# One 128x128 score product per block in the heads of gated linear attention

## The chip, the cores and the metric

The kernel runs on one core of one Trainium2 chip. The metric is the device time of one execution in microseconds, the median of several runs. TensorE (PE) multiplies matrices, VectorE (DVE), ScalarE (ACT) and GpSimd (POOL) work elementwise, SyncE (SP) issues transfers; each has a queue of its own and works through it in order.

## The reference, cut to what matters

One layer over 512 tokens of 1024 channels: a convolution branch and a branch of gated linear attention, merged, then a feed-forward part. The attention branch has 4 heads, 128 key channels and 256 value channels per head, in chunks of 64 tokens:

```
b = cumsum(gk) in the chunk          # log decay, per key channel
q_dec = q * exp(b);  k_inv = k * exp(-b);  k_end = k * exp(b_last - b)
att  = tril(q_dec @ k_inv.T)         # inside a chunk
o    = att @ v + q_dec @ state       # state: what the chunks before left
state = exp(b_last) * state + k_end.T @ v
o = rmsnorm(o) * silu(r)
```

The rest of the layer (norms, input projection, convolutions, feed-forward) is not touched.

## The kernel before, in words

**Weight products.** Nearly all of TensorE's work is products of the layer's weights in three parts (mm3, L444 to L450: activation low by weight high, high by low, high by high) with 512 tokens moving. A weight tile is loaded by SyncE, its high part made on ScalarE (L355, L385), its low part on VectorE (L356, L390) or, for some tiles, on ScalarE (L387) with an accumulating transfer issued by GpSimd (L388). Two tiles ahead are prepared (`weight`, L408). Pieces of the convolution branch (chains of taps on VectorE and ScalarE, L784 to L806) are put between weight tiles by `fill` (L428). A scheduler orders each engine's queue from the program.

**The heads.** The attention works on blocks of 128 tokens, two chunks each, four blocks. The loop (L1232) runs five rounds: a round prepares head h (decays, queries, keys) and finishes head h-1 (scores, states, outputs), with a weight product between each two of these steps; the outputs of head h-2 are turned and gated (`gated`, L1080) inside the scores of head h-1.

- `decays` (L990): a scan gives b, one buffer that all heads share; e = exp(b), inv = exp(-b), end = exp(b_last - b), three scratch tiles of 512 columns from a pool that rotates through 6 buffers (tag tmp). ea and eb are copies of e at the ends of the first and second chunk of each block (L1002, L1003), dec their product (L1004).
- `queries` (L1006): the tile q holds 4 slots of 64 per block. Slots 0 and 2 get q * e of both chunks (L1010), slot 1 the second chunk times ea (L1012). Slots 0 and 1 are the queries against the state before the block, slot 2 the second chunk's own.
- `keys` (L1014): the tile k holds 5 slots per block. Slots 0 and 2 get k * inv (L1017), slots 1 and 4 k * end (L1018), slot 3 slot 1 times eb (L1020). Slots 3 and 4 are the keys at the block's end, for the state.
- `scores` (L1022): four transposes of slots 3 and 4 (L1026) go through PSUM to kt (L1028). Then, per block, a 64x64 product of the first chunk with itself (L1035, keys slot 0, queries slot 0), and a product of both chunks' keys (slots 1 and 2) with the second chunk's queries (slot 2, L1037). All are f32. Two predicated copies (L1040) put the visible part into att: 64 rows by 128 columns, and 64 rows by 64 columns.
- `states` (L1042): three products of kt with v (L1050), summed with dec (L1054, L1057); the fourth block's keys in kt are not read.
- `outputs` (L1060): att with v (L1069), queries slots 0 and 1 with the state (L1071), squares for the norm (L1073), mean (L1075), its root on GpSimd (L500), the scaled output o (L1078). `gated` turns o (L1084), multiplies (L1087) and splits (L894, L895).

PSUM has five banks for weight products (mm) and three for the rest (ax), each set handed out in rotation. `gate_r` (L1092) runs a weight product and a Silu (L1095) between the steps; `spread` (L846, product in L850) and `token_sums` (L839) belong to the norm of the convolution branch and come later.

Of the kernel before, what the change touches and what calls it, by code (L numbers as in the profile page):

```python
# [10 lines left out]
F32 = mybir.dt.float32  # L11
# [3 lines left out]
AF = mybir.ActivationFunctionType  # L15
ALU = mybir.AluOpType

P = 128
D = 1024
T = 512  # L20
NT = T // P
# [54 lines left out]
def trunk_layer(ctx: ExitStack, tc: tile.TileContext, a: dict, out: bass.AP):  # L76
    nc = tc.nc
# [5 lines left out]
    def scoped(name, bufs, side="left"):  # L83
        scope = ExitStack()
        return scope, scope.enter_context(tc.tile_pool(name=name, bufs=bufs, side=side))
# [11 lines left out]
    gla_scope, gp = scoped("gla", 1, "right")  # L97
# [3 lines left out]
    def nm(s):  # L101
        return f"{s}_{next(names)}"

    def heap(dt=F32):
        return hp.tile([P, T], dt, tag="h", name=nm("h"))

    def tmp(n=T):
        return tp.tile([P, n], F32, tag="tmp", name=nm("tmp"), bufs=6)
# [7 lines left out]
    def small(n, tag):  # L116
        return tp.tile([P, n], F32, tag=tag, name=nm(tag), bufs=4)
# [4 lines left out]
    def ax_bank():  # L122
        return ps.tile([P, T], F32, tag="ax", name=nm("ax"), bufs=3)
# [6 lines left out]
    ident = cp.tile([P, P], F32, name="ident")  # L130
# [7 lines left out]
    keep = cp.tile([P, P], U8, name="keep")  # L138
    att = gp.tile([P, NT, P], F32, name="att")
# [98 lines left out]
    kept = {}  # L238
# [169 lines left out]
    def weight(name, j, ahead=LOOK):  # L408
        assert order[used[0]] == (name, j)
        prefetch(1)  # L410
        used[0] += 1
        prefetch(ahead)
        share = {"two": 2.5, "w_glu": RATE + 0.75}.get(name, RATE)

        fill(share + (1.75 if order[min(len(ready), len(order)) - 1] in ADDED else 0))
        return ready[used[0] - 1]
# [35 lines left out]
    def col_tile(w, acts, acc=None, lo=0, hi=T, at={}, ks=range(KT)):  # L452

        if acc is None:
            acc = mm_bank()
        for k in ks:
            s = slice(k * P, (k + 1) * P)
            ah, al = acts[k]
            mm3(acc[:, lo:hi], (w[0][:, s], w[1][:, s]), (ah[:, lo:hi], al[:, lo:hi]), k == 0, k == KT - 1)
            if k in at:  # L460
                at[k]()
        return acc
# [35 lines left out]
    def rsqrt(v, n):  # L498
        r = small(n, "rstd")
        roots_at[:] = [nc.gpsimd.tensor_tensor(r, v, mhalf[:, :n], ALU.pow)]  # L500
        return r
# [6 lines left out]
    def junk(n):  # L508
        return tp.tile([P, n], BF16, tag="junk", name=nm("junk"), bufs=1)
# [42 lines left out]
    start = tc.manual_schedule(engines=START)  # L552
    start.__enter__()
    rows = tp.tile([P, P], F32, tag="gain", name=nm("rows"), bufs=1)[0:KT, :]
# [261 lines left out]
    for k in range(KT):  # L816
# [3 lines left out]
        pa = col_tile(weight("w_glu", 2 * k), acts1)  # L820
        c = heap()
# [104 lines left out]
    rows = slice(32, 32 + RANK)  # L926
# [9 lines left out]
    rows = slice(96, 96 + RANK)  # L936
# [24 lines left out]
    def gl(n, tag, bufs):  # L961
        return gp.tile([P, n], F32, tag=tag, name=nm(tag), bufs=bufs)

    G16 = 1.0 / 16.0
    QS = float(np.float32(DK**-0.5))
    C = 64
    oa = [None] * KT

    def chunks(t):
        return t.rearrange("p (a c j) -> p a c j", c=2, j=C)  # L970

    def flat(t, p, i):
        return t[:, p, i : i + 2, :].rearrange("p c j -> p (c j)")

    def by_chunk(t):
        return t.rearrange("p (c j) -> p c j", j=C)

    class Head:
# [11 lines left out]
        def decays(self):  # L990
            b = gl(T, "b", 1)
            nc.vector.tensor_tensor_scan(b, run64, ls[self.h], 0.0, ALU.mult, ALU.add)
            self.e, self.inv, self.end = tmp(), tmp(), tmp()
            nc.scalar.activation(self.e, b, AF.Exp, scale=G16)
            nc.scalar.activation(self.inv, b, AF.Exp, scale=-G16)
            bc = by_chunk(b)
            last = bc[:, :, C - 1 : C].to_broadcast([P, 2 * NT, C])
            nc.vector.tensor_tensor(by_chunk(self.end), last, bc, ALU.subtract)
            nc.scalar.activation(self.end, self.end, AF.Exp, scale=G16)
            ends = chunks(self.e)[:, :, :, C - 1]  # L1000
            self.ea, self.eb, self.dec = small(NT, "ea"), small(NT, "eb"), small(NT, "dec")
            nc.vector.tensor_copy(self.ea, ends[:, :, 0])  # L1002
            nc.vector.tensor_copy(self.eb, ends[:, :, 1])  # L1003
            nc.vector.tensor_tensor(self.dec, self.ea, self.eb, ALU.mult)  # L1004

        def queries(self):  # L1006
            pq = col_tile(weight("w_qk", 2 * self.h), acts1)
            q = self.q = gp.tile([P, NT, 4, C], F32, tag="q", name=nm("q"), bufs=2)
            qc = q.rearrange("p a c j -> p (a c) j")[:, 0::2, :]
            nc.vector.scalar_tensor_tensor(qc, by_chunk(pq), QS, by_chunk(self.e), ALU.mult, ALU.mult)  # L1010
            ea = self.ea.unsqueeze(2).to_broadcast([P, NT, C])
            nc.vector.tensor_tensor(q[:, :, 1, :], q[:, :, 2, :], ea, ALU.mult)  # L1012

        def keys(self):  # L1014
            pk = col_tile(weight("w_qk", 2 * self.h + 1), acts1)
            k = self.k = gp.tile([P, NT, 5, C], F32, tag="k", name=nm("k"), bufs=2)
            nc.vector.tensor_tensor(k[:, :, 0:3:2, :], chunks(pk), chunks(self.inv), ALU.mult)  # L1017
            nc.vector.tensor_tensor(k[:, :, 1:5:3, :], chunks(pk), chunks(self.end), ALU.mult)  # L1018
            eb = self.eb.unsqueeze(2).to_broadcast([P, NT, C])
            nc.vector.tensor_tensor(k[:, :, 3, :], k[:, :, 1, :], eb, ALU.mult)  # L1020

        def scores(self, between=None):  # L1022
            q, k = self.q, self.k
            pt = ax_bank()
            for p in range(NT):
                nc.tensor.transpose(pt[:, p * P : (p + 1) * P], flat(k, p, 3), ident)  # L1026
            self.kt = gl(T, "kt", 1)
            nc.scalar.copy(self.kt, pt)  # L1028
            if between:
                between()  # L1030
            pa = ax_bank()
            pb = pa.rearrange("p (a i) -> p a i", a=NT)

            for p in range(NT):
                nc.tensor.matmul(pb[:C, p, :C], k[:, p, 0, :], q[:, p, 0, :], start=True, stop=True)  # L1035
            for p in range(NT):
                nc.tensor.matmul(pb[:, p, C:], flat(k, p, 1), q[:, p, 2, :], start=True, stop=True)  # L1037
            for rows, cols in ((slice(0, C), slice(0, P)), (slice(C, P), slice(C, P))):
                visible = keep[rows, cols].unsqueeze(1).to_broadcast([C, NT, cols.stop - cols.start])
                nc.vector.copy_predicated(att[rows, :, cols], visible, pb[rows, :, cols])  # L1040

        def states(self):  # L1042

# [16 lines left out]
        def outputs(self):  # L1060
            self.o = tp.tile([P, NT, DV], F32, tag="x", name=nm("o"), bufs=3)
            ss = small(NT, "ss4")
            halves = []
            for p in range(NT):
                if p % 2 == 0:
                    po = ax_bank()
                half = po[:, (p % 2) * DV : (p % 2 + 1) * DV]
                halves.append(half)
                nc.tensor.matmul(half, att[:, p, :], self.v(p), start=True, stop=p == 0)  # L1069
                if p:  # L1070
                    nc.tensor.matmul(half, flat(self.q, p, 0), self.s[p], start=False, stop=True)  # L1071
            for p, half in enumerate(halves):
                nc.scalar.activation(junk(DV), half, AF.Square, scale=1.0 / 16.0, accum_out=ss[:, p : p + 1])  # L1073
            v = small(NT, "mean")
            nc.vector.tensor_scalar(v, ss, EPS, None, ALU.add)  # L1075
            r = rsqrt(v, NT)
            for p, half in enumerate(halves):
                nc.scalar.activation(self.o[:, p, :], half, AF.Copy, scale=r[:, p : p + 1])  # L1078
# [526 lines left out]
    ends = {}  # L1605
# [21 lines left out]
    for gi, pairs in enumerate(GROUPS):  # L1627
        acts = []
        if gi == 0:
# [8 lines left out]
            p, q = pairs[0]  # L1638
# [139 lines left out]
```

## Time and profile before

| | |
|---|---|
| median of 3 runs | 824.66 us (824.33 to 824.96) |
| span of the profiled execution | 822.8 us |
| its own time beside the span | not given apart; the median lies 1.9 us above the span |
| instructions | 11563 |
| scan of the first head to L1084 of the last (the heads) | 149.4 to 284.8 us |
| HBM read, written | 103.42 MB, 2.10 MB |

The span runs from the first to the last instruction that the profiler saw. A row of the chain gives the start, the length that counts until the next step, the engine, the tile, the line and the number of passes. A row of the timeline gives start, duration, engine, line, operation, tile out and in, shapes, and in brackets the idle time ahead with what ended it. A row of groups gives count, total busy time, mean ns of one, and idle time ahead. TensorE's rows carry the form of its tile (128*64 is rows by columns of weights); a duration there includes the way through the pipeline, so the distance of two starts is what a pass costs. An f32 product shows as two passes.

### The profile page before, as it was taken

The numbers are of one execution on the slowest core, as the hardware profiler recorded it, in microseconds if no ns is written. First come the engines' busy times: TensorE is split into PE (matmuls) and PEld (weight loads), VectorE is DVE, ScalarE is ACT, GpSimd is POOL, SyncE is SP. The second block draws the span as 40 slices with busy tenths as digits, with TensorE's granted clock in tenths as the row PEclk, the third lists the DMA queues.
The fourth block names the chain that finished last, engine by engine and source line by source line (L and its number), as shares of the span: only waits on it lengthen the run. The fifth ranks groups of instructions, "written<-read, shape, count | busy, mean of one in ns | idle before, by whom it ended". The sixth has DMA issues, their size and how long they took to land.

```text
span 822.8 us, 11563 instructions
## 1 busy us (share of the span) xinstructions
PE 814.5 (99%) x4323; PEld 703.3 (85%) x4323; DVE 719.0 (87%) x1165; ACT 450.6 (55%) x666; POOL 146.5 (18%) x133
## 2 busy tenths in 40 slices
PE   9999999999999999999999999999999999999996
PEld 7888888888888889999988898898889988899885
DVE  6689999998989699876788889979975999789896
ACT  6643447656564446684445546556435663466654
POOL 2000010001100213532001000230133301612012
PEclk9999999999999999999999999999999999999999
DMA  8355572553432113223547623145632446224662
GB/s 317 104 131 147 146 192 83 129 154 102 106 100 103 51 35 120 103 78 122 206 107 222 192 73 103 45 161 160 141 137 83 147 129 165 105 103 147 186 128 103
DMA packets 30616, 106.27 MB, mean 129 GB/s; under 512 B 3464, under 2 KB 3600, under 8 KB 30560
## 3 DMA queue, kind: packets, MB, share of 16 engines
q1 hardware_dynamic: 24784, 85.34, 29.4%
q0 software_dynamic: 5760, 20.19, 14.1%
q8 instruction: 34, 0.56, 0.3%
q14 instruction: 22, 0.18, 0.1%
q10 hardware_dynamic: 16, 0.00, 0.0%
HBM read 103.42 MB, written 2.10 MB: 128 GB/s over the span
## 4 chain that ended last, share of the span: by engine, by line
PE 98%; DMA 1%; ACT 0%; DVE 0%; POOL 0%; issue 0%; POOLq 0%; SPq 0%; ACTq 0%
PE mm L448 28%; PE mm L449 28%; PE mm L450 28%; PE mm L662 3%; PE ax L450 2%; PE ax L449 2%; PE ax L448 2%; PE ax L1069 1%; PE ax L1071 1%; PE ax L1050 1%; DMA raw<-in_w_v_dram 1%; PE ax L1037 1%; PE ax L529 0%; PE ax L576 0%; PE ax L1035 0%; PE ax L1084 0%
## 5 line engine op out<-in xcount | busy, mean ns | idle before, releaser
L448 PE MATMUL mm<-uh,wlo 128*128 128x512 f32 (+1 forms) x672 | 244.5, 364 | 0.0
L449 PE MATMUL mm<-ul,whi 128*128 128x512 f32 (+1 forms) x672 | 242.3, 361 | 0.0
L450 PE MATMUL mm<-uh,whi 128*128 128x512 f32 (+1 forms) x672 | 242.1, 360 | 0.0
L450 PEld LDWEIGHTS mm<-uh,whi 128*128 128x128 f32 x672 | 126.8, 189 | 19.5
L448 PEld LDWEIGHTS mm<-uh,wlo 128*128 128x128 f32 x672 | 127.0, 189 | 18.8
L449 PEld LDWEIGHTS mm<-ul,whi 128*128 128x128 f32 x672 | 127.0, 189 | 18.6
L385 ACT CAST whi<-raw 128x1024 fp32r<-128x1024 f32 x86 | 89.9, 1048 | 56.2 <-PE mm L450 31.1
L356 DVE TENSOR_TENSOR wlo<-raw,whi 128x1024 fp32r<-128x1024 f32 x80 | 95.2, 1197 | 26.5 <-ACT whi L355 22.4
L327 POOL TENSOR_TENSOR raw<-raw,raw 128x512 f32<-128x512 f32 x42 | 66.7, 1589 | 215.8 <-DVE wlo L356 127.6
L390 DVE TENSOR_TENSOR wlo<-raw,whi 128x1024 fp32r<-128x1024 f32 x70 | 90.0, 1288 | 13.1 <-ACT whi L385 13.1
L355 ACT CAST whi<-raw 128x1024 fp32r<-128x1024 f32 x80 | 76.4, 959 | 36.5 <-PE mm L450 27.3
L788 DVE SCALAR_TENSOR_TENSOR c<-h,pp,c 128x255 f32<-128x255 f32 (+14 forms) x120 | 58.9, 491 | 3.2 <-ACT c L784 3.1
L788 DVE SCALAR_TENSOR_TENSOR c<-aside,btmp,c 128x255 f32<-128x255 f32 (+14 forms) x120 | 58.8, 490 | 0.0
L788 DVE SCALAR_TENSOR_TENSOR aside<-h,pp,aside 128x255 f32<-128x255 f32 (+6 forms) x112 | 54.9, 490 | 0.0
L355 ACT CAST whi<-kept 128x1024 fp32r<-128x1024 f32 (+1 forms) x32 | 31.8, 997 | 30.8 <-DVE kept L310 16.5
L1502 DVE SCALAR_TENSOR_TENSOR tmp<-mm,pp,tmp 128x511 f32<-128x511 f32 (+1 forms) x56 | 41.4, 742 | 4.0 <-ACT tmp L1499 3.9
L356 DVE TENSOR_TENSOR wlo<-kept,whi 128x1024 fp32r<-128x1024 f32 (+1 forms) x32 | 38.0, 1187 | 5.4 <-ACT whi L355 5.4
L1180 ACT COPY tmp<-mm 128x256 f32<-128x256 f32 x48 | 17.7, 369 | 35.9 <-PE mm L450 35.4
L1418 DVE TENSOR_TENSOR hres<-hres,mm 128x512 f32<-128x512 f32 (+1 forms) x49 | 32.3, 672 | 2.8 <-PE mm L450 2.0
L1499 ACT ACTIVATE tmp<-mm,pp 128x512 f32<-128x512 f32 x28 | 21.8, 779 | 19.0 <-PE mm L450 18.8
L387 ACT ACTIVATE wlo<-raw 128x1024 fp32r<-128x1024 f32 x16 | 16.9, 1060 | 22.1 <-PE mm L448 22.1
L1502 DVE SCALAR_TENSOR_TENSOR tmp<-tmp,pp,tmp 128x511 f32<-128x511 f32 (+1 forms) x32 | 27.8, 887 | 0.3
(351 smaller groups left out, 1778.6 us busy)
## 6 DMA issues: line engine op xcount, KB each, us to landing
raw<-in_w_up_dram SPq DMA_DIRECT2D x44, 512.0 KB, 3.6
raw<-in_w_glu_dram SPq DMA_DIRECT2D x16, 512.0 KB, 5.2
raw<-in_w_down_dram SPq DMA_DIRECT2D x15, 512.0 KB, 3.8
kept<-in_w_down_dram POOLq DMA_DIRECT2D x10, 512.0 KB, 5.5
raw<-in_w_v_dram SPq DMA_DIRECT2D x8, 512.0 KB, 5.5
raw<-in_w_qk_dram SPq DMA_DIRECT2D x8, 512.0 KB, 3.3
raw<-in_w_r_dram SPq DMA_DIRECT2D x8, 512.0 KB, 4.5
wlo<-in_w_r_dram POOLq DMA_DIRECT2D x8, 512.0 KB, 8.6
```

The source lines that it names most:

```text
L327: work = nc.gpsimd.tensor_tensor(out, x, y, ALU.add)
L355: nc.scalar.copy(hi, raw)
L356: two_low[:] = [nc.vector.tensor_tensor(lo, raw, hi.bitcast(F32), ALU.subtract)]
L385: nc.scalar.copy(hi, raw)
L390: pace[0] = nc.vector.tensor_tensor(lo, raw, hi.bitcast(F32), ALU.subtract)
L448: nc.tensor.matmul(acc, ll, rh, start=first, stop=False, **kw)
L449: nc.tensor.matmul(acc, lh, rl, start=False, stop=False, **kw)
L450: nc.tensor.matmul(acc, lh, rh, start=False, stop=last, **kw)
L662: nc.tensor.matmul(acc, act, ready[k // 2][wi][:, j], start=first, stop=last)
L788: nc.vector.scalar_tensor_tensor(out[:, j:], x[:, : half_t - j], w, out[:, j:], ALU.mult, ALU.add)
L1418: done = nc.vector.tensor_tensor(hres[t, n][:, c], hres[t, n][:, c], acc[:, c], op)
L1502: nc.vector.scalar_tensor_tensor(z[:, s:], acc[:, : T - s], w[j], z[:, s:], ALU.mult, ALU.add)
```

## The change

For a block's first chunk the queries are now also scaled from the chunk's end: q * exp(b) * exp(-b_last). With these, keys scaled to the first chunk's end serve the queries of both chunks, and one product of 128 keys by 128 queries gives a block's scores. The tile q gets the new slot 0; the old slots 0, 1 and 2 become 1, 2 and 3. The tile k loses the slot of the first chunk's k * inv. inv is computed from the last token of the first chunk on (65 of 128 columns per block). ea and eb are no copies any more but views of e. The keys of the last block are neither scaled for the state nor turned. The two predicated copies become one over 128 rows.

```diff
@@ -972,6 +972,9 @@
     def flat(t, p, i):
         return t[:, p, i : i + 2, :].rearrange("p c j -> p (c j)")
 
+    def by_block(t):
+        return t.rearrange("p (a i) -> p a i", a=NT)
+
     def by_chunk(t):
         return t.rearrange("p (c j) -> p c j", j=C)
 
@@ -992,52 +995,50 @@
             nc.vector.tensor_tensor_scan(b, run64, ls[self.h], 0.0, ALU.mult, ALU.add)
             self.e, self.inv, self.end = tmp(), tmp(), tmp()
             nc.scalar.activation(self.e, b, AF.Exp, scale=G16)
-            nc.scalar.activation(self.inv, b, AF.Exp, scale=-G16)
+            after_half = slice(C - 1, 2 * C)
+            nc.scalar.activation(by_block(self.inv)[:, :, after_half], by_block(b)[:, :, after_half], AF.Exp, scale=-G16)
             bc = by_chunk(b)
             last = bc[:, :, C - 1 : C].to_broadcast([P, 2 * NT, C])
             nc.vector.tensor_tensor(by_chunk(self.end), last, bc, ALU.subtract)
             nc.scalar.activation(self.end, self.end, AF.Exp, scale=G16)
             ends = chunks(self.e)[:, :, :, C - 1]
-            self.ea, self.eb, self.dec = small(NT, "ea"), small(NT, "eb"), small(NT, "dec")
-            nc.vector.tensor_copy(self.ea, ends[:, :, 0])
-            nc.vector.tensor_copy(self.eb, ends[:, :, 1])
+            self.ea, self.eb, self.dec = ends[:, :, 0], ends[:, :, 1], small(NT, "dec")
             nc.vector.tensor_tensor(self.dec, self.ea, self.eb, ALU.mult)
 
         def queries(self):
             pq = col_tile(weight("w_qk", 2 * self.h), acts1)
             q = self.q = gp.tile([P, NT, 4, C], F32, tag="q", name=nm("q"), bufs=2)
-            qc = q.rearrange("p a c j -> p (a c) j")[:, 0::2, :]
+            qc = q.rearrange("p a c j -> p (a c) j")[:, 1::2, :]
             nc.vector.scalar_tensor_tensor(qc, by_chunk(pq), QS, by_chunk(self.e), ALU.mult, ALU.mult)
             ea = self.ea.unsqueeze(2).to_broadcast([P, NT, C])
-            nc.vector.tensor_tensor(q[:, :, 1, :], q[:, :, 2, :], ea, ALU.mult)
+            nc.vector.tensor_tensor(q[:, :, 2, :], q[:, :, 3, :], ea, ALU.mult)
+            from_end = by_block(self.inv)[:, :, C - 1].unsqueeze(2).to_broadcast([P, NT, C])
+            nc.vector.tensor_tensor(q[:, :, 0, :], q[:, :, 1, :], from_end, ALU.mult)
 
         def keys(self):
             pk = col_tile(weight("w_qk", 2 * self.h + 1), acts1)
-            k = self.k = gp.tile([P, NT, 5, C], F32, tag="k", name=nm("k"), bufs=2)
-            nc.vector.tensor_tensor(k[:, :, 0:3:2, :], chunks(pk), chunks(self.inv), ALU.mult)
-            nc.vector.tensor_tensor(k[:, :, 1:5:3, :], chunks(pk), chunks(self.end), ALU.mult)
-            eb = self.eb.unsqueeze(2).to_broadcast([P, NT, C])
-            nc.vector.tensor_tensor(k[:, :, 3, :], k[:, :, 1, :], eb, ALU.mult)
+            k = self.k = gp.tile([P, NT, 4, C], F32, tag="k", name=nm("k"), bufs=2)
+            nc.vector.tensor_tensor(k[:, :, 0:4:3, :], chunks(pk), chunks(self.end), ALU.mult)
+            nc.vector.tensor_tensor(k[:, :, 1, :], chunks(pk)[:, :, 1, :], chunks(self.inv)[:, :, 1, :], ALU.mult)
+            kept = slice(0, NT - 1)
+            eb = self.eb[:, kept].unsqueeze(2).to_broadcast([P, NT - 1, C])
+            nc.vector.tensor_tensor(k[:, kept, 2, :], k[:, kept, 0, :], eb, ALU.mult)
 
         def scores(self, between=None):
             q, k = self.q, self.k
-            pt = ax_bank()
-            for p in range(NT):
-                nc.tensor.transpose(pt[:, p * P : (p + 1) * P], flat(k, p, 3), ident)
-            self.kt = gl(T, "kt", 1)
+            pt = ax_bank()[:, : T - P]
+            for p in range(NT - 1):
+                nc.tensor.transpose(pt[:, p * P : (p + 1) * P], flat(k, p, 2), ident)
+            self.kt = gl(T, "kt", 1)[:, : T - P]
             nc.scalar.copy(self.kt, pt)
             if between:
                 between()
             pa = ax_bank()
-            pb = pa.rearrange("p (a i) -> p a i", a=NT)
+            pb = by_block(pa)
 
             for p in range(NT):
-                nc.tensor.matmul(pb[:C, p, :C], k[:, p, 0, :], q[:, p, 0, :], start=True, stop=True)
-            for p in range(NT):
-                nc.tensor.matmul(pb[:, p, C:], flat(k, p, 1), q[:, p, 2, :], start=True, stop=True)
-            for rows, cols in ((slice(0, C), slice(0, P)), (slice(C, P), slice(C, P))):
-                visible = keep[rows, cols].unsqueeze(1).to_broadcast([C, NT, cols.stop - cols.start])
-                nc.vector.copy_predicated(att[rows, :, cols], visible, pb[rows, :, cols])
+                nc.tensor.matmul(pb[:, p, :], flat(k, p, 0), q[:, p, 0:4:3, :], start=True, stop=True)
+            nc.vector.copy_predicated(att, keep.unsqueeze(1).to_broadcast([P, NT, P]), pb)
 
         def states(self):
 
@@ -1068,7 +1069,7 @@
                 halves.append(half)
                 nc.tensor.matmul(half, att[:, p, :], self.v(p), start=True, stop=p == 0)
                 if p:
-                    nc.tensor.matmul(half, flat(self.q, p, 0), self.s[p], start=False, stop=True)
+                    nc.tensor.matmul(half, flat(self.q, p, 1), self.s[p], start=False, stop=True)
             for p, half in enumerate(halves):
                 nc.scalar.activation(junk(DV), half, AF.Square, scale=1.0 / 16.0, accum_out=ss[:, p : p + 1])
             v = small(NT, "mean")
```

The lines of the changed kernel lie a few further down: for example L1040 is the merged product, L1041 the predicated copy, L1031 the transposes.

## The prediction

> **What bounds the kernel now.** I read the busy line, then the chain that ended last, then what TensorE waited for.
>
> ```profile
> PE 814.5 (99%) x4323; PEld 703.3 (85%) x4323; DVE 719.0 (87%) x1165; ACT 450.6 (55%) x666; POOL 146.5 (18%) x133
> PE 98%; DMA 1%; ACT 0%; DVE 0%; POOL 0%; issue 0%; POOLq 0%; SPq 0%; ACTq 0%
> ```
>
> TensorE is busy in 99% of the span and makes 98% of the chain. The view of cores gives its clock, and the view of waits its longest wait on another engine after the start, for a low weight part:
>
> ```profile
> core 0: 822.8 us, clock 0.999
> PEld mm L449 <- DVE wlo L356: 0.2, 1, 0.2
> ```
>
> So the kernel is as long as TensorE's stream, at full clock, and the change is worth what it takes out of that stream, less what it makes TensorE wait.
>
> The chain in order of time shows a step of the heads at the length that counts (start, length, line, passes). Here is one step with its neighbours, the last step, and then, further on, the rstd spread of the conv branch (L850), whose shape I need.
>
> ```profile
> 201.79 0.44 PE ax L1026 x4
> 202.23 0.44 PE mm L1084 x4
> 202.67 0.44 PE ax L1084 x4
> 203.10 0.61 PE ax L1035 x8
> 203.71 1.03 PE ax L1037 x8
> 204.75 0.29 PE mm L448
> ...
> 261.48 0.61 PE ax L1035 x8
> 262.08 1.03 PE ax L1037 x8
> 263.12 0.29 PE mm L448
> ...
> 341.96 0.89 PE ax L850 x8
> 342.85 0.23 PE mm L448
> ```
>
> All four steps have these lengths; only the first has no L1084. The tile forms stand in the groups by form:
>
> ```profile
> L1037 PE MATMUL ax<-q,k 128*128 128x64 f32 x32 | 4.4, 281 | 0.0
> L1035 PE MATMUL ax<-q,k 128*64 128x64 f32 x32 | 2.7, 228 | 0.0
> L850 PE MATMUL ax<-ident,rstd 128*128 128x128 f32 x8 | 1.1, 274 | 0.0
> ```
>
> Each f32 product is two passes (x32 for 16 products). L1035 uses a 128*64 tile and 64 moving columns, L1037 the whole array and 64 columns. L850 is 128*128 weights with 128 moving columns, also f32: the merged product's shape.
>
> **The change, TensorE.** Removed per head: one transpose of four, 0.44/4 = 0.11 us; L1035, 0.61; L1037, 1.03; and the first product behind them at 0.29. Added: four products of L850's shape, 8 passes, 0.89, and the first product behind them at 0.23 as behind L850. That is 0.11 + 1.93 - 1.12 = 0.92 us per head, 3.68 us in four heads. The order of the built program confirms the rest of the stream: 3 transposes instead of 4, 4 products instead of 8 in each head, and everything else on TensorE in the old order, as on SyncE and GpSimd.
>
> Why do 8 passes with 64 columns take 1.03 when 8 with 128 take 0.89? The view of weight-load waits points at the change of tile form:
>
> ```profile
> PEld ax L1035 <- issue: 0.7, 4, 0.2
> ```
>
> Each head's first L1035 load stands for 0.2 us with nothing to wait for. After the change no product in the heads has the narrow tile. [...]
>
> One thing L850 does not show: the merged product's moving operand is two runs of 64 with a gap of 128 elements (q[:, p, 0:4:3]); no row has a moving operand with a gap. Bounds per pass: L850's 0.11 us, and L448's 0.23 us, a pass of 512 columns. Below 0.11 I see no row for this shape. At 0.23 the 8 passes take 1.84 and a head saves 0.11 + 1.93 - 1.84 - 0.23, so -0.03 us: about 0.1 us lost in all. I take 0.11: the runs are long and L850 is the same in all else. [...] The written scores stay contiguous here; only the read has the gap.
>
> **VectorE.** Removed per head: two copies of 4 elements, one of two 512-element key products, one of two predicated copies. Added: one key product of 256 elements, one query product of 256; L1020 shrinks from 256 to 192.
>
> ```profile
> L1018 DVE TENSOR_TENSOR k<-mm,tmp 128x512 f32<-128x512 f32 x4 | 2.7, 686 | 0.0
> L1040 DVE COPY_PREDICATED att<-keep,ax 64x256 f32<-64x256 uint8 x4 | 1.8, 452 | 0.1
> L1012 DVE TENSOR_TENSOR q<-q,ea 128x256 f32<-128x256 f32 x4 | 1.7, 431 | 0.0
> L1002 DVE COPY ea<-tmp 128x4 f32<-128x4 f32 x4 | 0.7, 178 | 0.0
> ```
>
> -0.69 - 0.45 + 0.43 + 0.43, -0.1 for L1020, -0.1 to -0.36 for the copies: about -0.5 to -0.7 us per head. The strided reads of ea and eb cost nothing that I count. ScalarE's inv shrinks from 512 to 260 elements and kt from 512 to 384. None of this is on the chain; it counts where TensorE, now up to 3.7 us early, meets a late result. Two places are near.
>
> **First place: o of the first head, read by the second step's L1084 (202.23 in the chain).** The scheduler moved things here: mean (L1075) now stands behind dec and the subtraction L998, and ScalarE does all three exponentials before o, the first of them even before the last square that mean needs.
>
> ```profile
> 194.78 1.23 DVE L992 TENSOR_TENSOR_SCAN b<-run,h 128x512 f32<-128x512 bf16 x1
> 195.91 0.41 DVE L802 TENSOR_TENSOR c<-c,aside 128x256 f32<-128x256 f32 x1
> 196.90 0.17 DVE L1075 TENSOR_SCALAR mean<-ss 128x4 f32<-128x4 f32 x1
> 200.90 0.69 DVE L998 TENSOR_TENSOR tmp<-b 128x512 f32<-128x512 f32 x1
> 197.15 1.54 POOL L500 TENSOR_TENSOR rstd<-mean,mhalf 128x4 f32<-128x4 f32 x1 [3.96 <-DVE mean L1075]
> 198.72 1.57 ACT L1078 ACTIVATE o<-ax,rstd 128x256 f32<-128x256 f32 x4 [2.06 <-POOL rstd L500]
> ```
>
> VectorE works without a pause here, so the scan comes earlier by its savings so far (two heads' products and one predicated copy, about 0.7 us): 194.1. It takes 1.13 to the next start; three operations stand now between 195.91 and 196.90, 0.33 each. After the change five stand there, then dec (0.18) and L998 (0.69): mean at 194.1 + 1.13 + 1.65 + 0.87 = 197.75, 0.85 later than now. (Its last square is done before that: the scan ends at 195.3, and one exponential and one square take about 1.2.) o's four quarters then run from 199.55 to 201.15. TensorE reaches L1084 at 202.23 - 0.92 - 0.11 = 201.2 and takes a quarter per 0.11 us. Slack about 0.1 to 0.4 us. I charge nothing; if the cover is gone it costs what o is late.
>
> **Second place: an added wait.** Scratch tiles rotate through six buffers, and e and inv now live until the key products. The fourth head's inv (L995) takes the buffer of the third head's e, whose last reader is now L1020 of that head instead of L1010. In the built order this L995 gained a wait on VectorE. Behind it on ScalarE stand a weight's high part (1.04), a table load (1.28), the gate's Silu (0.60) and the four squares that give mean its input.
>
> ```profile
> 210.94 1.04 ACT L385 CAST whi<-raw 128x1024 fp32r<-128x1024 f32 x1
> 212.00 1.28 ACT L1095 ACT_TABLE_LOAD   x1
> 217.08 0.60 ACT L1095 ACTIVATE h<-mm 128x512 f32<-128x512 f32 x1 [3.80 <-PE mm L450]
> ...
> 216.68 0.42 DVE L1020 TENSOR_TENSOR k<-k,eb 128x256 f32<-128x256 f32 x1
> 225.47 0.17 DVE L1075 TENSOR_SCALAR mean<-ss 128x4 f32<-128x4 f32 x1
> 226.95 1.57 ACT L1078 ACTIVATE o<-ax,rstd 128x256 f32<-128x256 f32 x4 [4.97 <-POOL rstd L500]
> ...
> L1073 ACT ACTIVATE junk<-ax 128x256 bf16<-128x256 f32 x16 | 6.2, 385 | 3.3 <-PE ax L1071 3.1
> L1073 ACT ACTIVATION_READ_ACCUMULATOR junk<-ax 128x1 f32 x16 | 3.2, 200 | 0.0
> ```
>
> Taking L1020 as late as now, 217.1, ScalarE needs 0.3 + 1.04 + 1.28 + 0.60, four squares with their reads (4 x 0.59) and two more weight operations (2 x 1.04): 224.8, still ahead of mean at 225.47. ScalarE's idle times of 3.80 and 4.97 us hide it. o would end at 228.5; TensorE wants it at 231.4 - 2 x 0.92 - 0.11 = 229.4. Slack 0.9 us at worst; VectorE's earlier finish adds to it.
>
> **Does the gain last?** After the heads VectorE waits for TensorE:
>
> ```profile
> 279.56 0.17 DVE L1075 TENSOR_SCALAR mean<-ss 128x4 f32<-128x4 f32 x1 [1.79 <-ACT junk L1073]
> 284.39 1.41 DVE L1087 SCALAR_TENSOR_TENSOR tmp<-ax,pp,h 128x512 f32<-128x512 f32 x2 [4.66 <-PE ax L1084]
> ```
>
> Even if VectorE gained only 2 us to TensorE's 3.7, its idle 4.66 us shrinks to 3.0 and it is released by TensorE as before. From there every engine follows TensorE, so all the rest moves forward as one.
>
> **The sum.** The profiled span is 822.8 us; the median of the runs is 824.66, 1.9 us more, which I keep. 824.66 - 3.68 = 820.98, say 821.0.
>
> **Rivals.**
> A. Full-width weights, not the tile switch, make L1037's pass 1.03/8 = 0.13 us, and the merged pass costs the same. A head saves 0.11 + 0.61 = 0.72, in all 2.9: 821.8. For it: the load is the same 128 columns. Against it: L850's 0.11 with the same load. Chance 0.10.
> B. The gap in the moving operand slows the pass, and the change doesn't give what its merged product promises. At twice 0.11, 8 passes take 1.78: 0.11 + 1.93 - 1.78 - 0.23 = 0.03 us per head, 824.5; at 0.23, 824.8. For it: no row shows such an operand. Against it: runs of 64. [...] Chance 0.05.
> C. A stall of 0.5 to 1.4 us at the first place, because mean now stands behind dec and L998: 821.5 to 822.4. For it: slack under 0.4. Against it: VectorE's backlog shrinks too. Chance 0.11.
> D. Slower: the added wait at the second place. From L1020's end beyond 218.0 (217.1 + 0.9) each us costs TensorE one us; beyond 218.0 + 3.7 = 221.7 the gain is gone, and beyond 221.7 + 1.65 = 223.35 the kernel is slower by more than 0.2%: 826.5 at 223.5. For it: one in-order queue now hangs on another, VectorE, that is busy 87% of the span. Against it: VectorE has less to do. Chance 0.02.
>
> **How the numbers follow.** The forecast with its small errors (0.15 us per head, some tenths of run to run) has 0.72: 820.3 to 821.6. A and C make 0.21, B 0.05, D 0.02. The range 820.2 to 822.4 takes in A and nearly all of C; outside stay B, D and a little on the low side. 0.2% of 824.66 is 1.65 us, about what a measurement here tells from no change: faster means below 823.0. Faster 0.93, same 0.05 (B), slower 0.02 (D).
>
> **What would show it.** Right: merged score passes at 0.89 per 8 in the chain and 0.23 behind them; no issue wait of the weight loads in the heads; L448's next tile 0.92 us earlier after the first step, 3.7 after the last; no new TensorE wait over 0.3 us. Wrong: 1.03 or more for the 8 passes (A, B); TensorE waiting for o (ScalarE L1078) at L1084 of the second or third step (C, D).

## The result, and the profile after

The changed kernel took 820.92 us (median, 820.65 to 821.81) beside 824.96 us for the kernel before in the same comparison: a ratio of 0.9954, 95% interval 0.9942 to 0.9966. The forecast was 821.0, worked from 824.66 us for the kernel before. A second comparison on another chip gave 821.68 beside 824.68, ratio 0.9960 (0.9946 to 0.9974). The two differences, 4.0 and 3.0 us, lie on both sides of the 3.68 that were forecast, so the runs alone don't measure the change to better than half a microsecond. The chain, read below, does. The profiled execution of the changed kernel had a time of its own of 820.78 us, with a span of 818.9.

The busy line, the shares of the chain and the view of cores, of the changed kernel:

```profile
PE 810.3 (99%) x4287; PEld 700.5 (86%) x4287; DVE 715.6 (87%) x1157; ACT 448.9 (55%) x666; POOL 148.8 (18%) x133
PE 98%; DMA 1%; ACT 0%; DVE 0%; POOL 0%; issue 0%; POOLq 0%; SPq 0%; ACTq 0%
core 0: 818.9 us, clock 0.999
```

TensorE still sets the time, and at the same clock. It is busy 4.2 us less, VectorE 3.4 us less, and ScalarE, whose inv and kt shrank, 1.7 us less. Only the first of the three should show in the time.

The chain of the changed kernel in order of time (start, length, line, passes): the start of the first head's step, the second step, a pair of passes that is needed further down, the weight product behind the last step, and the last turning of o.

```profile
173.46 0.33 PE ax L1031 x3
...
200.85 0.33 PE ax L1031 x3
201.18 0.44 PE mm L1085 x4
201.61 0.44 PE ax L1085 x4
202.05 0.89 PE ax L1040 x8
...
216.47 0.45 PE ax L1070 x2
...
259.48 0.24 PE mm L448
...
280.21 0.87 PE ax L1085 x8
```

Two rows of the same view of the kernel before bound the same stretch:

```profile
173.48 0.44 PE ax L1026 x4
...
283.91 0.87 PE ax L1084 x8
```

From the first head's first transpose to the last turning of o TensorE took 283.91 - 173.48 = 110.43 us before and 280.21 - 173.46 = 106.75 after: 3.68 us less, 0.92 per head. The second step starts 201.79 - 200.85 = 0.94 us earlier, 0.02 of which the first one had already; the weight product behind the last step starts 263.12 - 259.48 = 3.64 us earlier. This **stretch of the heads** is the measure for the experiments below. It repeats to some hundredths: the second profile of the changed kernel gave 106.70.

The spans differ by 3.9, 0.2 more than the stretch. That is not the change. Far behind the heads one weight load of L448 stood for 0.3 us in the kernel before and not in the one after. The same load waits in five of the fourteen profiles of this document, up to 1.0 us in that of stride8 (an edit of the kernel after, below). The views of waits of the kernel before and of stride8:

```profile
PEld mm L448 <- issue: 0.3, 1, 0.3
PEld mm L448 <- ACT whi L385: 1.0, 1, 1.0
```

The chain names no cause in the kernel before, but the timelines lead to a transfer. The load stands behind an addition on VectorE (`hres`, L1418 in the kernel before), this one behind a weight's low part in VectorE's queue (L356), and that one behind the high part of the same weight on ScalarE (L355), which starts when the transfer of the weight has landed. Here it is in stride8, 2.05 us ahead of the load (700.46), and in the changed kernel, 3.08 us ahead of it (695.63):

```profile
698.41 0.62 ACT L355 CAST whi<-kept 128x512 fp32r<-128x512 f32 x1 [1.97 <-DMA kept<-in_w_down_dram]
692.55 0.62 ACT L355 CAST whi<-kept 128x512 fp32r<-128x512 f32 x1 [0.20 <-DMA kept<-in_w_down_dram]
```

In the kernel before, too, the high part starts 2.06 us ahead of the load (697.57 and 699.63). There the profile names a VectorE operation as what the high part waited for, one that ended 0.05 us behind the landing (697.52 and 697.47). So in these profiles the wait goes with the landing of one transfer, and the median of every kernel here may hold some of it.

After the heads, the changed kernel's timeline of VectorE:

```profile
275.85 0.17 DVE L1076 TENSOR_SCALAR mean<-ss 128x4 f32<-128x4 f32 x1 [1.79 <-ACT junk L1074]
280.68 1.41 DVE L1088 SCALAR_TENSOR_TENSOR tmp<-ax,pp,h 128x512 f32<-128x512 f32 x2 [4.66 <-PE ax L1085]
```

Both idle times are those of the kernel before, 1.79 and 4.66 us, and both rows stand 3.71 us earlier. VectorE is as far ahead of TensorE there as before, and the gain lasts.

### The profile page after: what moved, and what is told of

The parts are those of the page before. It is cut to its first block, busy times and chain, and to the rows that moved or that the text cites. A ratio compares the mean times of both kernels' runs of the same rounds, so it can differ in the third digit from the quotient of the medians.

```text
span 818.9 us, 11480 instructions
## 1 busy us (share of the span) xinstructions
PE 810.3 (99%) x4287; PEld 700.5 (86%) x4287; DVE 715.6 (87%) x1157; ACT 448.9 (55%) x666; POOL 148.8 (18%) x133
## 4 chain that ended last, share of the span: by engine, by line
PE 98%; DMA 1%; ACT 0%; DVE 0%; POOL 0%; issue 0%; POOLq 0%; SPq 0%; ACTq 0%
PE mm L448 28%; PE mm L449 28%; PE mm L450 28%; PE mm L662 3%; PE ax L450 2%; PE ax L448 2%; PE ax L449 2%; PE ax L1070 1%; PE ax L1072 1%; PE ax L1051 1%; DMA raw<-in_w_v_dram 1%; PE ax L1040 0%; PE ax L529 0%; PE ax L576 0%; PE ax L1085 0%; PE mm L933 0%
## 5 line engine op out<-in xcount | busy, mean ns | idle before, releaser
L448 PE MATMUL mm<-uh,wlo 128*128 128x512 f32 (+1 forms) x672 | 244.4, 364 | 0.0
L448 PEld LDWEIGHTS mm<-uh,wlo 128*128 128x128 f32 x672 | 127.0, 189 | 18.8
L356 DVE TENSOR_TENSOR wlo<-raw,whi 128x1024 fp32r<-128x1024 f32 x80 | 93.1, 1171 | 24.4 <-ACT whi L355 20.5
L355 ACT CAST whi<-raw 128x1024 fp32r<-128x1024 f32 x80 | 76.3, 957 | 34.8 <-PE mm L450 27.2
L355 ACT CAST whi<-kept 128x1024 fp32r<-128x1024 f32 (+1 forms) x32 | 31.8, 996 | 31.8 <-DVE kept L310 17.0
L356 DVE TENSOR_TENSOR wlo<-kept,whi 128x1024 fp32r<-128x1024 f32 (+1 forms) x32 | 36.8, 1153 | 4.8 <-ACT whi L355 4.7
```

The source lines that it names most:

```text
L355: nc.scalar.copy(hi, raw)
L356: two_low[:] = [nc.vector.tensor_tensor(lo, raw, hi.bitcast(F32), ALU.subtract)]
L448: nc.tensor.matmul(acc, ll, rh, start=first, stop=False, **kw)
```

## The experiments

Three questions: what the 0.92 us of a head are made of, what the gap in the moving operand costs, and how far the two places (and others) are from making TensorE wait. All twelve runs in one table (four_again repeats four_turns, and after_again repeats the changed kernel). "Stretch" is the stretch of the heads as above, with its change against the profile of the kernel named.

| kernel | edit of | time, us | ratio to before (95%) | stretch, us | change of stretch |
|---|---|---|---|---|---|
| wide64 | before | 824.97 | 1.0002 (0.9993 to 1.0011) | 110.75 | +0.32 |
| interleaved | before | 828.22 | 1.0042 (1.0027 to 1.0057) | 113.84 | +3.41 |
| three_turns | before | 824.30 | 0.9995 (0.9985 to 1.0004) | 109.98 | -0.45 |
| four_turns | after | 823.18 | 0.9977 (0.9967 to 0.9987) | 107.20 | +0.45 |
| four_again | after | 821.46 | 0.9959 (0.9943 to 0.9975) | 107.16 | +0.41 |
| contiguous | after | 821.42 | 0.9956 (0.9942 to 0.9969) | 106.94 | +0.19 |
| runs8 | after | 820.78, one run | | 106.79 | +0.04 |
| stride2 | after | 821.09, one run | | 106.85 | +0.10 |
| stride8 | after | 825.26 | 1.0002 (0.9993 to 1.0011) | 110.57 | +3.82 |
| copies | after | 821.42 | 0.9957 (0.9945 to 0.9970) | 107.27 | +0.52 |
| late_mean | after | 822.54 | 0.9971 (0.9959 to 0.9982) | 108.25 | +1.50 |
| after_again | after | 821.68 | 0.9960 (0.9946 to 0.9974) | 106.70 | -0.05 |

### What the 0.92 us are made of

**wide64**, on the kernel before: the first chunk's product takes the full-width weights.

```diff
-                nc.tensor.matmul(pb[:C, p, :C], k[:, p, 0, :], q[:, p, 0, :], start=True, stop=True)
+                nc.tensor.matmul(pb[:, p, :C], flat(k, p, 0), q[:, p, 0, :], start=True, stop=True)
```

> The kernel before, with one edit: the product of the first chunk (L1035) takes the whole 128-column weight tile, so that no product in the heads has the narrow form; it does more arithmetic than before, and the number of passes stays 8 and 8. Theory of the switch (a change of tile form costs 0.1 to 0.2 us each way, a full-width load costs nothing more than 0.11 us per pass): L1035's 8 passes 0.89, L1037's 8 passes 0.89 instead of 1.03, the product behind them 0.23 instead of 0.29, no issue wait of the weight load: 2.01 instead of 1.93 us per head, +0.1 per head, +0.3 us in all, about 825.0. Rival (full-width weights with 64 moving columns cost 0.13 us per pass, no price of the switch): 1.03 and 1.03, and 0.29 behind: 2.35 per head, +0.42, +1.7 us in all, 826.3.

The chain of wide64, second head:

```profile
203.24 0.84 PE ax L1035 x8
204.08 0.89 PE ax L1037 x8
204.98 0.29 PE mm L448
```

Line 1037 itself was not touched, and its 8 passes fell from 1.03 to 0.89 because the product ahead of it has no narrow tile any more. The issue wait of the loads is gone too. 0.84 + 0.89 + 0.29 = 2.02 against 0.61 + 1.03 + 0.29 = 1.93: +0.09 per head, as the theory of the switch has it; full-width weights are not what made L1037 slow. One part missed: 0.29 stayed behind the scores, so those 0.06 us have nothing to do with the tile form. The 0.84, 0.89 and the 0.06 make 1.79, 16 times 0.112: a pass costs the same 0.11 us throughout, and by this sum the 0.06 belong to the last 64-column pass.

**interleaved**, on the kernel before: the two products alternate block by block.

```diff
             for p in range(NT):
                 nc.tensor.matmul(pb[:C, p, :C], k[:, p, 0, :], q[:, p, 0, :], start=True, stop=True)
-            for p in range(NT):
                 nc.tensor.matmul(pb[:, p, C:], flat(k, p, 1), q[:, p, 2, :], start=True, stop=True)
```

> The kernel before, with L1035 and L1037 issued in turn, block by block, in one loop instead of two: the same 16 passes, but 8 changes of tile form in a head instead of 2. Theory of the switch: the price per change is (0.61 - 8 x 0.058 = 0.15) into the narrow form and (1.03 - 0.89 = 0.14) out of it, so 6 more changes cost about 0.9 us per head, 3.5 us in all: about 828. Rival (the passes with full-width weights are slow by themselves, 0.13 us each, and a change of form costs nothing): no change, 824.7.

The chain of interleaved, second head (L1036 is what was L1037):

```profile
204.27 0.26 PE ax L1035 x2
204.53 0.37 PE ax L1036 x2
...
206.76 0.29 PE mm L448
```

The 16 passes take 206.76 - 204.27 = 2.49 us instead of 1.64: the same work in the same number of passes, with 8 changes of tile form instead of 2. The six more cost 0.85, 0.14 us each, and the time rose by 3.56 us where 3.5 were expected. This is the plainest of the runs: a change of the tile form has a price of its own.

**three_turns** (on the kernel before) and **four_turns** (on the kernel after) move the fourth transpose alone.

```diff
-            pt = ax_bank()
-            for p in range(NT):
+            pt = ax_bank()[:, : T - P]
+            for p in range(NT - 1):
...
-            self.kt = gl(T, "kt", 1)
+            self.kt = gl(T, "kt", 1)[:, : T - P]
```

four_turns is the same edit backwards, with the fourth block of slot 2 scaled again by eb.

> The kernel before, with only 3 of the 4 transposes of the keys and a key tile of 384 columns copied by ScalarE. Theory of TensorE's stream: -0.11 us per head, -0.44 in all, 824.2. Rival (the transposes lie in a wait of TensorE for something else): no change, 824.7.

> The kernel after, with the fourth transpose, the fourth block of the decayed keys and the copy of 512 columns put back. Theory of TensorE's stream: +0.11 us per head, +0.44 in all, 821.4. Rival (the product alone makes the gain, the transposes lie in a wait): no change, 820.9.

The stretches moved by -0.45 and +0.45 us, 0.11 per head and transpose. On TensorE, what is left between the kernel before and four_turns is the merged product alone, 110.43 - 107.20 = 3.23 us, 0.81 per head. The time of three_turns, 0.36 us lower, agrees, but its interval holds no change: alone this part could not have been measured by the clock. The times of four_turns missed. Two executions, 821.27 (the profiled one) and 821.47, stood where they should, and seven stood between 823.0 and 823.9. four_again, the same kernel on another chip, was to catch one of these in a profile, beside after_again:

> The kernel with four transposes again, for a profile of its second group of times. Theory (a result of VectorE or ScalarE reaches TensorE with no slack in one of the heads, and a small lateness there is answered by a longer one): the profile shows TensorE's steps 1.5 to 2.5 us later from one point in the heads on, with a wait there. Rival (the second group has nothing to do with the heads: a DMA or a weight load elsewhere): the steps of the heads stand as in the first profile, and the lateness begins behind them. If the profile falls in the first group (821.4) it tells nothing.

> The kernel after, unchanged, on the chip on which the next three run, as their measure, and to see whether its times fall into two groups as those of the kernel with four transposes did (821.3 to 821.5 and 823.0 to 823.9). Theory (only four transposes have the second group): 820.7 to 821.8. Rival (the kernel after has it too, and it was not seen in five runs): some of the runs at 822.5 or more.

It did not: 821.33, 821.46 and 821.48, and the steps of the heads as in the first profile. The changed kernel ran from 820.76 to 822.0, with no time near 823. What held those seven executions for 2 us is open; no profile shows one. For the same reason the price of the fourth transpose rests on the chain, not on the medians. The load behind the heads is a place where executions differ, but its longest wait in a profile is 1.0 us.

**The sum.** Per head: the transpose 0.11; two changes of form at 0.14, 0.28; and the rest of what the products saved, 0.81 - 0.28 = 0.53, for eight passes less. Four heads: 0.44 + 1.12 + 2.12 = 3.68. The 0.53 are the eight narrow passes, which start 0.058 us apart in the trace of the kernel before (8 x 0.058 = 0.46), and the 0.06 behind the last 64-column pass. Most of the gain is simply the smaller number of passes.

### What the gap costs

**contiguous**, on the kernel after: the parts of the queries in another order, so that the operand of the merged product is one run of 128.

```diff
-            qc = q.rearrange("p a c j -> p (a c) j")[:, 1::2, :]
-            nc.vector.scalar_tensor_tensor(qc, by_chunk(pq), QS, by_chunk(self.e), ALU.mult, ALU.mult)
+            for c in range(2):
+                at = (slice(None), slice(None), c)
+                nc.vector.scalar_tensor_tensor(q[:, :, 3 * c, :], chunks(pq)[at], QS, chunks(self.e)[at], ALU.mult, ALU.mult)
...
-                nc.tensor.matmul(pb[:, p, :], flat(k, p, 0), q[:, p, 0:4:3, :], start=True, stop=True)
+                nc.tensor.matmul(pb[:, p, :], flat(k, p, 0), flat(q, p, 2), start=True, stop=True)
```

> The kernel after, with the four parts of the queries laid out in another order, so that the moving operand of the merged product is one run of 128 elements instead of two runs of 64 with a gap (and the operand of L1072 too is contiguous); the scaling of the queries takes two VectorE operations of 256 elements instead of one of 512. Theory (the gap costs nothing): the merged passes stay at 0.89 per 8, the time is the same within 0.2 us, 820.9. [...]

**runs8, stride2 and stride8**, on the kernel after: the moving operand has 128 elements as before, in 16 runs of 8 with gaps of 8, at every second element, or at every eighth. The edit of stride8; the other two change the same line.

```diff
+            spread_q = q.rearrange("p a c j -> p (a c j)")
             for p in range(NT):
-                nc.tensor.matmul(pb[:, p, :], flat(k, p, 0), q[:, p, 0:4:3, :], start=True, stop=True)
+                nc.tensor.matmul(pb[:, p, :], flat(k, p, 0), spread_q[:, p : 2 * T : 8], start=True, stop=True)
```

> The kernel after, with the merged product's moving operand read from the same queries at every eighth element (32 bytes apart, 128 columns). The scores are then not those of the reference: the queries are mixed; the number and size of the products are kept. Theory (the gap of the change costs nothing because a read from SBUF at any stride keeps pace): 0.89 per 8 passes, 820.9. Rival (a gap is free only because the runs are of 64 elements; a read without runs is slow): a pass goes from 0.11 to 0.23 us or more, 8 passes 1.8 or more, +0.9 per head, +3.7 us or more in all, 824.6 or more.

> The kernel after, with the merged product's moving operand read at every second element of the block's queries (8 bytes apart, 128 columns). The scores are then not those of the reference; the number and size of the products are kept. Theory (what costs is that single elements lie apart, whatever the distance): 1.86 per 8 passes as at every eighth element, 824.8. Rival (the cost follows the bytes that are run over: 1024 per partition for 128 columns here, 4096 there): 8 passes 0.89 to 1.1, 821 to 821.8.

> The kernel after, with the merged product's moving operand read as 16 runs of 8 elements with gaps of 8 (32 bytes on, 32 bytes off; 128 columns). The scores are then not those of the reference; the number and size of the products are kept. Theory (runs hide the gap, as the runs of 64 do): 0.89 per 8 passes, 821. Rival (runs as short as 8 pay part of what single elements pay): between 1.0 and 1.86 per 8 passes, 821.4 to 824.8.

The chains, second head, of contiguous (its scores are L1041), runs8, stride2 and stride8:

```profile
202.34 0.89 PE ax L1041 x8
```

```profile
202.18 0.89 PE ax L1041 x8
```

```profile
202.44 0.91 PE ax L1041 x8
```

```profile
203.09 1.86 PE ax L1041 x8
```

One run of 128, two of 64, sixteen of 8: 0.89 each. The gap of the change costs nothing, and closing it gains nothing. Elements 8 bytes apart (stride2, 0.91) cost 0.02 per eight passes; elements 32 bytes apart (stride8, 1.86) double the pass, from 0.11 to 0.23 us. The theory with which stride2 was sent, that single elements lying apart are what costs, falls: it matters how far apart they lie, and its rival (by the bytes run over) stands, with points at 8 and 32 bytes only. The time of stride8 lies 4.3 us above that of the changed kernel, 0.5 more than its stretch; its profile has the 1.0 us wait of the load behind the heads.

contiguous took 0.19 us more in the heads all the same. Its chain has it at one place, the third head's outputs, 0.63 for a pair of passes that takes 0.43:

```profile
216.76 0.63 PE ax L1071 x2
```

### How near a wait is

**copies**, on the kernel after: ea and eb are copies again, so that e is not held until the keys are made.

```diff
-            self.ea, self.eb, self.dec = ends[:, :, 0], ends[:, :, 1], small(NT, "dec")
+            self.ea, self.eb, self.dec = small(NT, "ea"), small(NT, "eb"), small(NT, "dec")
+            nc.vector.tensor_copy(self.ea, ends[:, :, 0])
+            nc.vector.tensor_copy(self.eb, ends[:, :, 1])
```

> The kernel after, with the two 4-element decays ea and eb copied out of e again, as before the change. The key product then does not read e, and the inverse decay of the fourth head on ScalarE does not wait for it any more, for two more VectorE copies of 0.18 us per head. Theory (the added wait is hidden, and VectorE is off the path): the same within 0.2 us, 820.9. Rival (the added wait costs something): faster by what it costs, at most some tenths; a VectorE on the path instead would be slower by 4 x 0.36 = 1.4 us, 822.3.

Neither came out as written. The medians don't tell copies and the changed kernel apart (ratios of 0.9957 beside 0.9954 and 0.9960), but the chain says that the heads lost 0.52 us, through two waits of TensorE. Not having to wait for e brought nothing; the copies make VectorE's results late elsewhere. The chain of copies at the second head's turning of o (L1087), and at the third head's outputs:

```profile
201.17 0.43 PE mm L1087 x3
201.60 0.04 issue
201.64 0.33 PE mm L1087
201.96 0.44 PE ax L1087 x4
...
216.81 0.61 PE ax L1072 x2
```

Four passes of the mm product take 201.96 - 201.17 = 0.79 us instead of 0.44: 0.35 lost, waiting for o. The timeline of copies has the reason:

```profile
197.73 0.17 DVE L1078 TENSOR_SCALAR mean<-ss 128x4 f32<-128x4 f32 x1
200.01 1.57 ACT L1081 ACTIVATE o<-ax,rstd 128x256 f32<-128x256 f32 x4 [1.53 <-POOL rstd L500]
```

Compare the changed kernel there, scan to o:

```profile
193.77 1.21 DVE L995 TENSOR_TENSOR_SCAN b<-run,h 128x512 f32<-128x512 bf16 x1
196.56 0.15 DVE L1006 TENSOR_TENSOR dec<-tmp 128x4 f32<-128x4 f32 x1
196.64 0.68 DVE L1002 TENSOR_TENSOR tmp<-b 128x512 f32<-128x512 f32 x1
197.24 0.16 DVE L1076 TENSOR_SCALAR mean<-ss 128x4 f32<-128x4 f32 x1
197.48 2.00 POOL L500 TENSOR_TENSOR rstd<-mean,mhalf 128x4 f32<-128x4 f32 x1 [5.23 <-DVE mean L1076]
199.52 1.57 ACT L1079 ACTIVATE o<-ax,rstd 128x256 f32<-128x256 f32 x4 [1.53 <-POOL rstd L500]
```

o starts 0.49 us later with the copies and TensorE, which is there at the same time (201.17 and 201.18), loses 0.35. So the changed kernel has about 0.49 - 0.35 = 0.14 us to spare at this place.

The other 0.18 us of copies (0.61 for 0.43) is the wait that contiguous has. In the changed kernel it is just beginning. Its timeline:

```profile
214.56 1.22 DVE L390 TENSOR_TENSOR wlo<-raw,whi 128x1024 fp32r<-128x1024 f32 x1
215.69 0.48 DVE L1058 SCALAR_TENSOR_TENSOR state<-state,dec,ax 128x256 f32<-128x256 f32 x1
216.22 0.30 PEld L1070 LDWEIGHTS ax<-h,att 128*128 128x128 f32 x2 [0.15 <-DVE state L1058]
```

Compare the kernel before:

```profile
217.01 0.48 DVE L1057 SCALAR_TENSOR_TENSOR state<-state,dec,ax 128x256 f32<-128x256 f32 x1
217.40 1.22 DVE L390 TENSOR_TENSOR wlo<-raw,whi 128x1024 fp32r<-128x1024 f32 x1
...
217.97 0.41 PEld L1069 LDWEIGHTS ax<-h,att 128*128 128x128 f32 x2
```

Before, the state's first update stood ahead of a weight's low part on VectorE and was done at 217.49, 0.48 us ahead of the load at 217.97. After, the two have changed places and the update ends at 216.17, with the load behind it at 216.22. On the chain the pair of passes takes 0.45 (the row at 216.47 above) instead of 0.43; in after_again it takes 0.43. In contiguous and copies the update starts 0.47 and 0.51 us later (216.16 and 216.20), but TensorE too reaches the pair 0.29 and 0.34 us later (216.76 and 216.81). Against TensorE the update is only 0.18 and 0.17 us later, and the pair takes 0.20 and 0.18 longer: there is no slack here.

**late_mean**, on the kernel after: one more VectorE operation of 0.43 us in each head.

```diff
             nc.vector.tensor_tensor(self.dec, self.ea, self.eb, ALU.mult)
+            nc.vector.tensor_tensor(by_chunk(self.inv)[:, 1::2, :], by_chunk(self.inv)[:, 1::2, :], by_chunk(self.inv)[:, 1::2, :], ALU.max)
```

> The kernel after, with one more VectorE operation in each head (256 elements of the inverse decay, the maximum with itself, about 0.42 us, behind dec), so that mean and o of the first head come later. It adds work and leaves the result as it is. Theory (the o of the first head had a slack of a few tenths at the second step's product, L1085): with 0.4 to 0.8 us of lateness, depending on how many of these operations stand ahead of mean, TensorE waits there 0.1 to 0.7 us, and the time grows by that, 821.0 to 821.6. Rival (the slack is over 0.8 us): the same, 820.9.

It did not test what it was made for. The scheduler took mean ahead, to 196.70 us, and o was early. What it did is worth seeing. Its timeline around the new operation (L1007):

```profile
203.31 0.42 ACT L999 ACTIVATE tmp<-b 128x260 f32<-128x260 f32 x1
203.76 0.43 DVE L1007 TENSOR_TENSOR tmp<-tmp 128x256 f32<-128x256 f32 x1 [2.39 <-ACT tmp L999]
204.10 1.22 DVE L995 TENSOR_TENSOR_SCAN b<-run,h 128x512 f32<-128x512 bf16 x1
```

and its view of weight-load waits:

```profile
PEld ax L1052 <- DVE tmp L1089: 1.3, 1, 1.3
PEld ax L1071 <- DVE state L1059: 0.5, 1, 0.5
```

VectorE stood 2.39 us for an inverse decay that ScalarE made only behind o, a Silu and two table loads; the next scan stands at 204.10 instead of 197.42 in the changed kernel. From there VectorE ran without a pause and late into two things that TensorE reads, and the heads lost 1.50 us.

The kernel before has such a pause too, and the changed kernel a shorter one, behind its early scan (VectorE's rows, before and after):

```profile
204.17 1.23 DVE L992 TENSOR_TENSOR_SCAN b<-run,h 128x512 f32<-128x512 bf16 x1 [2.58 <-ACT tmp L995]
203.52 0.48 DVE L788 SCALAR_TENSOR_TENSOR c<-aside,btmp,c 128x255 f32<-128x255 f32 x1 [1.40 <-ACT c L784]
```

Before, the pause delayed nothing, because TensorE came later. With TensorE earlier it counts: late_mean, with the longer pause and the added operations, keeps 110.43 - 108.25 = 2.18 of the 3.68 us. So part of the gain seems to hang on the order that the scheduler found for the changed kernel; how much of the loss is the pause and how much the added work was not separated.

None of the experiments points to a faster version: without the wait at the state the changed kernel would gain 0.02 us, and the layout without the gap gains nothing.

## Why the prediction was right, point by point

- **TensorE sets the time, at full clock.** Right: 99% busy and 98% of the chain on both sides.
- **0.92 us per head on TensorE.** Right in the sum and in its terms: three transposes 0.33, the merged passes 0.89 per eight as L850's, 0.24 behind them for 0.23. That the time itself came within 0.1 us of 820.98 is partly luck: the kernel before stood 0.3 us higher in this comparison than in the forecast, and the difference of the medians was 4.0.
- **The change of tile form.** The place was right and the prediction's account fell short. It had 0.2 us of issue wait. The runs give the price, 0.14 us for each change of form (0.85 for six more in interleaved), two per head: 1.12 of 3.68 us. What inside TensorE takes that time, no run shows. What the account left out is most of the gain: a pass with 128 weight columns costs 0.11 us with 64 or 128 moving columns (0.84 and 0.89 per eight in wide64, 0.89 in the changed kernel), so that the full-width product took on the first chunk's columns at no cost, and the eight narrow passes went. The sum used the lengths on the chain and not this account, and so did not suffer.
- **Rival A** (full-width weights are slow) fell: 0.89, and wide64's L1037 at 0.89 with 64 columns.
- **The gap** was taken at L850's price, and that is what it costs. **Rival B** fell here, though a gap can slow the pass: stride8 pays 0.23 per pass, the upper bound that was taken from L448. Two runs of 64, runs of 8 (0.89 each) and every second element (0.91) were as fast as one run of 128 or within 0.02 us per eight passes, and only every eighth element was slow (1.86).
- **The first place.** No wait, as forecast, and 0.14 us of slack where 0.1 to 0.4 were given. The working had two errors that cancelled. mean was to come at 197.75 and came at 197.24: the scan 0.33 earlier than thought, and dec and the subtraction counted with their durations (0.87) where the distance of starts is what counts (197.24 - 196.56 = 0.68). Then GpSimd's root took 2.00 us where the row taken from before had 1.54. o came at 199.52 for 199.55. That the forecast of o holds is luck. **Rival C** did not happen in the changed kernel; copies shows its mechanism at 0.35 us.
- **The second place** was misread. The fourth head's inv (now L999) was to wait for the third head's L1020 (now L1025). In the changed kernel it ran well ahead of it. ScalarE's row and VectorE's row:

```profile
210.26 0.42 ACT L999 ACTIVATE tmp<-b 128x260 f32<-128x260 f32 x1
...
213.96 0.35 DVE L1025 TENSOR_TENSOR k<-k,tmp 128x192 f32<-128x192 f32 x1
```

  It has no idle time in front of it. In late_mean, where VectorE is late, the same operation waits 0.59 us, for L895, an earlier reader of a scratch tile. Which operation the changed kernel's wait hangs on was not settled; if it is L895 there too (it ends at 209.17), there is 1.1 us to spare. The place costs nothing, as forecast, but not by the forecast's working, and **rival D**, built on L1025, had no ground.
- **A third place was missed**: the third head's state, L1058, which the scheduler put behind a weight's low part. It has no slack at all, 0.02 us lost in one profile and none in the other. That it cost nothing is luck: each further tenth by which VectorE is late against TensorE there is lost (0.18 us late cost 0.20 in contiguous), and no rival named it.
- **The gain lasts.** Right: the idle 4.66 us after the heads is whole, where the forecast allowed for 3.0.

## What to carry to other kernels

Where TensorE sets the time, count passes and changes of tile form before multiplications: one product with full-width weights and 128 moving columns replaced two with 64 moving columns and gave 0.81 us of 1.93, though it computes more. Take the cost of a moved piece from a row of the same form and shape, and lay it out by the distance of starts, not by durations. And when TensorE moves ahead, go through every small result that it reads in the stretch (o, the states, the split weights), because a scheduler reorders the queue of the engine that makes it: half a microsecond here decided whether a place (o) cost nothing or 0.35 us.

## What the runs showed of the hardware that was not expected

- An f32 pass with full-width weights costs 0.11 us with 64 moving columns (0.84 and 0.89 per eight in wide64) as with 128 (0.89), while one with 64 weight columns starts 0.058 us behind the one ahead of it (the passes of L1035 in the kernel before). With 64 moving columns in both, the pass with half the weight columns took about half the time.
- A change of tile form between 128*128 and 128*64 costs 0.14 us (0.85 for six more in interleaved), more than a pass of either form (0.11 and 0.058).
- The distance of the elements that a moving operand reads can double a pass: 0.11 us with f32 elements 8 bytes apart (stride2, 0.91 per eight), 0.23 at 32 bytes (stride8, 1.86 per eight).
- The same 4-column root on GpSimd took 1.54 us in the kernel before and 2.00 in the kernel after, at the same place of the program. In the changed kernel and in copies it takes 2.00, and VectorE's next scan runs beside it (from 197.42 and 197.92); in the kernel before and in late_mean it takes 1.54, and that scan comes only at 204.17 and 204.10. That the scan is the cause is not shown by a run made for it.
